# Tying the later modulation's multiplications behind a retention step's own VectorE work

## The chip, the cores and the metric

The kernel runs on one core of one Trainium2 chip. The metric is the device time of one execution in microseconds (us), and lower is better. A core has five engines that run side by side, each through its own queue of instructions in a fixed order: TensorE (PE in the profile, with its weight loads as PEld), VectorE (DVE), ScalarE (ACT), GpSimd (POOL) and SyncE (SP), which here issues most of the DMAs. An engine that waits for a semaphore holds up everything behind the waiting instruction in its own queue.

## The reference, cut to what matters

The reference is one block of a network on 2048 tokens of width 1024. A modulation vector is computed from a conditioning vector `c`, and it is cut into six parts that shift, scale and gate the two halves of the block. The first half mixes tokens with eight heads: four gated linear recurrences (HGRN2) and four retention heads. The second half is a feed-forward part with a short convolution.

```
mod_x = silu(c) @ w_mod + b_mod            # 6 x 1024 values
sh1, sc1, g1, sh2, sc2, g2 = split(mod_x, 6)
hx = rmsnorm(x, norm1_g) * (1 + sc1) + sh1
...                                        # retention, chunk by chunk, per head:
scores = (q_chunk @ k_chunk.T) * intra
o      = scores @ v_chunk + (q_chunk * q_dec) @ r
r      = chunk_dec * r + (k_chunk * k_dec).T @ v_chunk
...
x = x + g1 * (mixed @ w_out)
hx2 = rmsnorm(x, norm2_g) * (1 + sc2) + sh2
x = x + g2 * conv_ffn(hx2)
```

Only `sh1` and `sc1` are needed before the heads. The other four parts, `g1`, `sh2`, `sc2` and `g2`, are needed after them.

## The kernel before, in words

The modulation is computed in twelve stripes of 512 columns. Stripes 0 to 3 (`sh1`, `sc1`) are made at the start. Stripes 4 to 11 are made later, by `mod_later`, while the retention heads run. A stripe is a sum over 1024 rows of `w_mod`, and its rows come in eight tiles of 128 rows. VectorE multiplies each tile by a column of `silu(c)` and adds it to the accumulator `macc` (lines 287 and 289), which is one `tensor_scalar` and seven `scalar_tensor_tensor` for a stripe. Then `mod_rows` sums over the 128 partitions with four small TensorE products (line 232), and line 235 adds the bias. `macc` has one buffer, so a stripe begins when the stripe before it has been summed up. The tiles `wm` have four buffers (tag `q`), so the load of a tile (line 278, on SyncE's queue) waits until the tile four before it has been multiplied.

The heads run one after the other, `h` from 0 to 7, and the last four are retention heads (4 to 7). Each head goes through four steps `i` of 512 tokens. A step (written (h, i) below) weaves three things together: `ret_sweep1` of this head, `ret_sweep2` of the head before it, and the projection `ret_proj` for the next step. In `ret_sweep1`, TensorE makes the scores `rsc` (line 1201), VectorE multiplies them with the decay into `rA` (line 1203), TensorE makes four state increments `rup` (line 1119), and then the running state is carried through four chunks: TensorE multiplies with the state (`rob`, line 1221), and VectorE makes the next state (`Kt`, and `rSb` for the last chunk, line 1223). After this line 1227 scales and adds. In `ret_proj`, TensorE's long products `pa`, `pb`, `pc` are taken from PSUM by lines 578 and 586 (VectorE) and by ScalarE; the query and key are then turned by position: a DMA swaps partitions, GpSimd multiplies by the sine (line 1188), and VectorE does lines 1191 and 1192, without which the next step's `rsc` cannot start.

`tick` is called twice in a step, once after the first three pieces of `ret_sweep1` and once at its end. It runs the compute parts whose loads the tick before has started, and starts the next loads. In heads 4, 5 and 6 a tick takes two weight items (preparation of the next head's weights, line 644 among others) and two items of `mod_later`. An item is two tiles. So half a stripe is written down at each tick: stripe 4 at the second tick of (4, 0) and the first of (4, 1), stripe 5 at the second of (4, 1) and the first of (4, 2), stripe 6 at the second of (4, 2) and in the flush ahead of (4, 3). Head 5 does the same with stripes 7, 8 and 9, and head 6 with stripes 10 and 11, which end at the first tick of (6, 2).

The order in which a tick is written down is not the order on the engine. The framework's scheduler plays the program through a timing model of its own while it builds it, and puts an instruction on its engine's queue when the model says that it can start; of several that can start, the one written down first goes first. An instruction whose inputs are ready early can so be queued ahead of work that was written down before it. `issue_after(ins)` adds an edge to each instruction of its block that runs on the engine of `ins`: it is queued behind `ins`. It adds no wait on the chip, since an engine works in the order of its queue. The kernel has one such edge already, at line 1190: line 1191 is queued behind the last `whole` of the projection.

Of the kernel before, what the change touches and what calls it, by code (L numbers as in the profile page):

```python
# [15 lines left out]
ALU = mybir.AluOpType  # L16
PSUM = bass.MemoryType.PSUM

P = 128
# [27 lines left out]
def view(t, off, dims):  # L47
    return bass.AP(t.tensor, t.offset + off, [t.ap[0]] + dims)


class Kern:
# [215 lines left out]
    def mod_later(self, j4):  # L267

        nc = self.nc
        wsrc = self.I["w_mod"][0].rearrange("(k p) n -> p k n", p=P)  # L270
        st = {}

        def item(k0):
            def load():

                st[k0] = w = [self.slot_tile([P, 512], F32, "q", "wm") for _ in range(2)]
                for kk in range(2):
                    nc.sync.dma_start(w[kk], wsrc[:, k0 + kk, 512 * j4:512 * j4 + 512])

            def comp():  # L280
                if k0 == 0:
                    st["acc"] = self.slot_tile([P, 512], F32, "FG", "macc")
                acc, w = st["acc"], st[k0]
                for kk in range(2):
                    c = self.silc[:, k0 + kk:k0 + kk + 1]
                    if k0 + kk == 0:
                        ins = nc.vector.tensor_scalar(acc, w[kk], c, None, ALU.mult)
                    else:
                        ins = nc.vector.scalar_tensor_tensor(acc, w[kk], c, acc, ALU.mult, ALU.add)

                if k0 + 2 == KT:
                    self.mod_rows(acc, 1, j4)
            return load, comp
        return [item(k0) for k0 in range(0, KT, 2)]
# [900 lines left out]
    def ret_sweep1(self, pool, h, g, slot, pr, st):  # L1195
        nc = self.nc
        qk, V = pr["qk"], pr["V"]
        sc = self.ps("sc", [P, 4, P], "rsc")
        for c in range(4):
            cs = slice(c * P, (c + 1) * P)  # L1200
            nc.tensor.matmul(sc[:, c], qk[:, 1, cs], qk[:, 0, cs], start=True, stop=True, skip_group_check=True)
        A = pool.tile([P, 4, P], F32, tag="A", bufs=2, name="rA")
        nc.vector.tensor_tensor(A, sc, view(self.Dm, h * P, [[0, 4], [1, P]]), ALU.mult)
        yield
        Kt = self.slot_tile([P, 2, 4, P], F32, "KTt", "Kt")
        ups = yield from self.ret_increments(h, qk[:, 1], V, Kt)
        ou, qf = self.slot_tiles(slot)
        nc.scalar.copy(qf, qk[:, 0])
        Uf = ou[:, 1].rearrange("p (c t) -> p c t", t=P)
        for i in range(2):  # L1210
            nc.scalar.copy(Uf[:, 2 * i:2 * i + 2], ups[i][:, :, 0])
        op = self.ps("sc", [P, 4, P], "rop")
        for c in range(4):
            nc.tensor.matmul(op[:, c], A[:, c], V[:, c], start=True, stop=True, skip_group_check=True)
        opart = ou[:, 0].rearrange("p (c t) -> p c t", t=P)
        nc.scalar.copy(opart, op)
        yield
        ob = self.ps("sc", [P, 4, P], "rob")
        Sb = st["Sb"]
        for c in (3, 2, 1, 0):  # L1220
            nc.tensor.matmul(ob[:, c], qk[:, 0, c * P:(c + 1) * P], Sb, start=True, stop=True, skip_group_check=True)
            S2 = Kt[:, 0, c] if c else pool.tile([P, P], F32, tag="S1", bufs=2, name="rSb")
            nc.vector.scalar_tensor_tensor(S2, Sb, self.cd[:, 1, h:h + 1], ups[c // 2][:, c % 2, 1], ALU.mult, ALU.add)
            Sb = S2
            yield
        st["Sb"] = Sb
        nc.vector.scalar_tensor_tensor(opart, ob, self.qd[:, 1, h:h + 1], opart, ALU.mult, ALU.add)
        st["grp"][g] = dict(qf=qf, Uf=Uf, T128=view(self.cd, h, [[NH, 2], [0, 4]]), op=opart)
# [607 lines left out]
```

## Time and profile before

| | us |
|---|---|
| runs of the kernel | 2736.52, 2742.63, 2743.33 (median 2742.63) |
| profiled execution | 2745.74 |
| its span, first to last instruction | 2743.7 |
| PE busy | 2562.4 (93%) |
| DVE busy | 1835.8 (67%) |
| ACT busy | 1343.5 (49%) |
| POOL busy | 773.9 (28%) |

Times in the profile count from the start of the span. A row of the timeline has the start, the duration, the engine, the line, the operation, what is written and read, the shape, and in brackets how long the engine sat idle before it and which instruction or DMA ended that. A row of the table by stretches has the busy time of each engine with the number of instructions, then the clock granted to TensorE as a share of 2.4 GHz (its other level, 1.2 GHz, is 0.50), then the share of time in which the DMA engines were busy, and GB/s.

### The profile page before, as it was taken

How to read it: one execution, taken by the hardware profiler on the slowest of the kernel's cores; microseconds unless marked ns; L12 is line 12 of the kernel's file. 1: busy time of each engine (PE TensorE's matmuls, PEld its weight loads, DVE VectorE, ACT ScalarE, POOL GpSimd, SP SyncE). 2: the span in 40 equal slices, each digit the busy share in tenths (PEclk: the TensorE clock that was granted, in tenths of full speed). 3: DMA queues.
4: the chain of work that ended last, by engine and by line, in shares of the span. 5: the costliest groups of instructions: out<-in, count | busy, mean ns of one | idle time of the engine just before them, and what ended most of it. 6: DMA issues, size and time to landing. Idle time of an engine off the chain costs nothing.

```text
span 2743.7 us, 56410 instructions
## 1 busy us (share of the span) xinstructions
PE 2562.4 (93%) x22829; PEld 1692.0 (62%) x22829; DVE 1835.8 (67%) x3569; ACT 1343.5 (49%) x2902; POOL 773.9 (28%) x905
## 2 busy tenths in 40 slices
PE   5789998999998989898999899999999999999998
PEld 2678887889888888787445344444444444444443
DVE  4998676775856666547464888778877777423553
ACT  5776456564544434336354665555555554411220
POOL 3742111220312132121244344344434433000101
PEclk7899999999999999999999999999999999999999
DMA  8224333343447766666532132333233234734552
GB/s 294 102 86 155 123 103 121 101 129 109 148 159 224 227 212 204 215 181 219 194 110 78 50 123 100 112 115 101 99 115 103 98 110 161 272 144 169 207 192 100
DMA packets 216693, 402.37 MB, mean 147 GB/s; under 512 B 16623, under 2 KB 98771, under 8 KB 211824
## 3 DMA queue, kind: packets, MB, share of 16 engines
q1 hardware_dynamic: 203808, 373.42, 40.1%
q10 hardware_dynamic: 12320, 25.18, 3.1%
q8 instruction: 178, 2.92, 0.4%
q14 instruction: 83, 0.68, 0.1%
q0 software_dynamic: 304, 0.17, 0.0%
HBM read 298.57 MB, written 91.75 MB: 142 GB/s over the span
## 4 chain that ended last, share of the span: by engine, by line
PE 63%; DVE 17%; DMA 7%; issue 6%; ACT 4%; POOL 3%; ACTq 0%; DVEq 0%; SPq 0%; POOLq 0%
PE pa L84 7%; PE pa L85 7%; PE pa L86 7%; PE pd L84 5%; PE pd L86 5%; PE pd L85 5%; PE pc L84 3%; PE pc L85 3%; PE pc L86 3%; PE pb L84 2%; PE pb L86 2%; PE pb L85 2%; PE opp L85 2%; PE opp L84 2%; PE opp L86 2%
## 5 line engine op out<-in xcount | busy, mean ns | idle before, releaser
L84 PE MATMUL pa<-feat,w 128*128 128x512 f16 x704 | 267.7, 380 | 8.6 <-ACT ta L544 8.0
L85 PE MATMUL pa<-feat,w 128*128 128x512 f16 x704 | 267.3, 380 | 1.1 <-DVE feat L1367 1.1
L86 PE MATMUL pa<-feat,w 128*128 128x512 f16 x704 | 263.9, 380 | 0.0
L85 PE MATMUL pd<-wd,actl 128*128 128x512 f16 x616 | 233.3, 379 | 0.0
L86 PE MATMUL pd<-wd,actl 128*128 128x512 f16 x616 | 233.3, 379 | 0.0
L84 PE MATMUL pd<-wd,actl 128*128 128x512 f16 x616 | 232.6, 379 | 0.1
L85 PEld LDWEIGHTS <-w 128*128 128x128 f16 x1232 | 120.8, 98 | 152.7 <-issue 12.9
L86 PEld LDWEIGHTS <-w 128*128 128x128 f16 x1232 | 121.4, 99 | 149.1 <-DVE w L644 2.9
L84 PEld LDWEIGHTS <-w 128*128 128x128 f16 x1232 | 121.7, 99 | 140.8 <-issue 1.6
L85 PEld LDWEIGHTS <-hx 128*128 128x128 f16 x1824 | 184.6, 101 | 11.7 <-issue 9.7
L86 PEld LDWEIGHTS <-hx 128*128 128x128 f16 x1824 | 184.6, 101 | 3.0 <-issue 1.9
L84 PEld LDWEIGHTS <-hx 128*128 128x128 f16 x1824 | 184.6, 101 | 2.4
L1592 DVE SCALAR_TENSOR_TENSOR st<-act,modT,st 128x512 f16<-128x512 f32 x154 | 142.9, 957 | 31.6 <-ACT st L1591 30.7
L84 PE MATMUL pa<-w_vg,hx 128*128 128x128 f16 x800 | 148.2, 224 | 5.5 <-DVE cb L578 4.6
L86 PE MATMUL pa<-w_vg,hx 128*128 128x128 f16 x800 | 148.2, 225 | 0.0
L85 PE MATMUL pa<-w_vg,hx 128*128 128x128 f16 x800 | 148.2, 224 | 0.0
L1591 ACT ACTIVATE st<-act,modT 128x512 f16<-128x512 f32 x154 | 107.5, 718 | 80.9 <-DVE act L1581 29.3
L86 PE MATMUL pc<-feat,w 128*128 128x512 f16 x352 | 134.1, 381 | 2.4 <-DVE w L644 2.4
L84 PE MATMUL pc<-feat,w 128*128 128x512 f16 x352 | 133.9, 380 | 2.3 <-ACT feat L1366 1.3
L85 PE MATMUL pc<-feat,w 128*128 128x512 f16 x352 | 133.9, 380 | 0.0
L84 PE MATMUL pa<-hx,w_z 128*128 128x256 f16 x464 | 128.7, 277 | 4.6 <-DVE K L586 2.1
L85 PEld LDWEIGHTS <-w_z 128*128 128x128 f16 x1072 | 108.7, 101 | 34.9 <-issue 23.0
(550 smaller groups left out, 7576.4 us busy)
## 6 DMA issues: line engine op xcount, KB each, us to landing
hx<-hxd SPq DMA_DIRECT2D x212, 512.0 KB, 5.0
actd<-st SPq DMA_DIRECT2D x154, 256.0 KB, 2.0
actl<-actd SPq DMA_DIRECT2D x28, 1024.0 KB, 5.1
wur<-in_w_up_dram SPq DMA_DIRECT2D x44, 512.0 KB, 4.1
raw<-in_w_in_dram SPq DMA_DIRECT2D x36, 512.0 KB, 4.3
wm<-in_w_mod_dram SPq DMA_DIRECT2D x64, 256.0 KB, 4.7
hxd<-hx SPq DMA_DIRECT2D x28, 512.0 KB, 3.4
wdb<-in_w_down_dram SPq DMA_DIRECT2D x44, 256.0 KB, 4.0
```

Of the source, the lines that this page charges most:

```text
L84: mm(ps, lhs(0), rhs(0), start=start, stop=False, skip_group_check=True)
L85: mm(ps, lhs(0), rhs(1), start=False, stop=False, skip_group_check=True)
L86: mm(ps, lhs(1), rhs(0), start=False, stop=stop, skip_group_check=True)
L1591: nc.scalar.activation(p[:, 0], v, AF.Copy, scale=s)
L1592: nc.vector.scalar_tensor_tensor(p[:, 1], v, s, p[:, 0], ALU.mult, ALU.subtract)
```

## The change

The two multiplications of an item are put in an `issue_after` block. The instruction that they are tied to is kept in `self.mark`. `ret_sweep1` sets it when it writes down line 1203 (`rA`), and again at each of the four state updates of line 1223. At the first tick of a step the mark is therefore this step's `rA`, and at the second tick its last state update `rSb`. In the flush ahead of (h, 3) it is the `rSb` of (h, 2). Line numbers after the first hunk move on by one.

```diff
                 acc, w = st["acc"], st[k0]
-                for kk in range(2):
-                    c = self.silc[:, k0 + kk:k0 + kk + 1]
-                    if k0 + kk == 0:
-                        ins = nc.vector.tensor_scalar(acc, w[kk], c, None, ALU.mult)
-                    else:
-                        ins = nc.vector.scalar_tensor_tensor(acc, w[kk], c, acc, ALU.mult, ALU.add)
-
+
+                with self.tc.issue_after(self.mark.ins):
+                    for kk in range(2):
+                        c = self.silc[:, k0 + kk:k0 + kk + 1]
+                        if k0 + kk == 0:
+                            nc.vector.tensor_scalar(acc, w[kk], c, None, ALU.mult)
+                        else:
+                            nc.vector.scalar_tensor_tensor(acc, w[kk], c, acc, ALU.mult, ALU.add)
                 if k0 + 2 == KT:
                     self.mod_rows(acc, 1, j4)
...
-        nc.vector.tensor_tensor(A, sc, view(self.Dm, h * P, [[0, 4], [1, P]]), ALU.mult)
+        self.mark = nc.vector.tensor_tensor(A, sc, view(self.Dm, h * P, [[0, 4], [1, P]]), ALU.mult)
...
-            nc.vector.scalar_tensor_tensor(S2, Sb, self.cd[:, 1, h:h + 1], ups[c // 2][:, c % 2, 1], ALU.mult, ALU.add)
+            self.mark = nc.vector.scalar_tensor_tensor(S2, Sb, self.cd[:, 1, h:h + 1], ups[c // 2][:, c % 2, 1], ALU.mult, ALU.add)
```

## Rows read from the trace of the kernel before

**Rows 1.** The table by stretches: the stage in which the later modulation is multiplied (from the last step of the HGRN2 heads into the first step of head 7), and the last half of the kernel. Columns: stretch, its length, PE, PEld, DVE, ACT and POOL busy (instructions), granted clock, DMA share, GB/s.

```profile
770.70:1220.00 449.30, 402.92 (x4802) 378.56 (x4800) 267.06 (x516) 182.99 (x463) 96.45 (x112) 0.95 0.66 208
1370.00:2743.70 1373.70, 1349.23 (x6640) 628.23 (x6638) 913.61 (x1512) 631.27 (x1133) 427.49 (x447) 0.99 0.37 128
```

**Rows 2.** The same table by step, from one `rA` to the next: from (4, 1) to (4, 2), with stripe 5 in it, and from (6, 0) to (6, 1), with no stripe in it.

```profile
830.20:864.87 34.67, 29.83 (x337) 28.06 (x336) 21.06 (x38) 14.63 (x34) 10.17 (x11) 0.95 0.69 213
1058.60:1090.39 31.79, 31.79 (x411) 30.76 (x410) 17.12 (x43) 13.80 (x40) 4.36 (x7) 1.00 0.51 159
```

**Rows 3.** The view of the tile `macc`: the multiplications (least, median and longest in ns, first and last start in us), and what VectorE waited for ahead of them (us in all, times).

```profile
L289 DVE SCALAR_TENSOR_TENSOR macc<-wm,silc,macc x56: 733/750/1751, 785.8 to 1115.9; 128x512 f32<-128x512 f32 x56
L287 DVE TENSOR_SCALAR macc<-wm,silc x8: 468/480/2471, 784.6 to 1103.0; 128x512 f32<-128x512 f32 x8
  DMA wm<-in_w_mod_dram: 21.7, 13
```

**Rows 4.** The timeline of VectorE in step (4, 1): a multiplication of stripe 5, and the first and the last state update of the step.

```profile
852.15 0.75 DVE L289 SCALAR_TENSOR_TENSOR macc<-wm,silc,macc 128x512 f32<-128x512 f32 x1 [4.20 <-DMA wm<-in_w_mod_dram]
852.82 0.34 DVE L1223 SCALAR_TENSOR_TENSOR Kt<-rSb,cd,rup 128x128 f32<-128x128 f32 x1
...
853.96 0.35 DVE L1223 SCALAR_TENSOR_TENSOR rSb<-Kt,cd,rup 128x128 f32<-128x128 f32 x1
```

**Rows 5.** The same in step (6, 1), with stripe 11.

```profile
1110.51 0.75 DVE L289 SCALAR_TENSOR_TENSOR macc<-wm,silc,macc 128x512 f32<-128x512 f32 x1 [4.69 <-DMA wm<-in_w_mod_dram]
...
1112.38 0.34 DVE L1223 SCALAR_TENSOR_TENSOR Kt<-rSb,cd,rup 128x128 f32<-128x128 f32 x1
...
1114.29 0.35 DVE L1223 SCALAR_TENSOR_TENSOR rSb<-Kt,cd,rup 128x128 f32<-128x128 f32 x1
```

**Rows 6.** The timeline of TensorE: the instructions of the stage that ended idle time of TensorE and stand near a stripe.

```profile
853.21 0.87 PE L1221 MATMUL rob<-Kt,K 128*128 128x128 f32 x4 [4.45 <-DVE Kt L1223]
...
894.80 1.79 PE L1201 MATMUL rsc<-K 128*128 128x128 f32 x8 [4.32 <-DVE K L1192]
...
978.10 0.49 PE L1221 MATMUL rob<-Kt,K 128*128 128x128 f32 x2 [1.29 <-DVE Kt L1223]
979.50 0.87 PE L1221 MATMUL rob<-Kt,K 128*128 128x128 f32 x4 [0.90 <-DVE Kt L1223]
...
1023.99 1.37 PE L1201 MATMUL rsc<-K 128*128 128x128 f32 x8 [1.25 <-DVE K L1192]
...
1048.35 0.22 PE L84 MATMUL pa<-w_vg,hx 128*128 128x128 f16 x1 [2.06 <-DVE cb L578]
...
1112.78 0.80 PE L1221 MATMUL rob<-Kt,K 128*128 128x128 f32 x2 [5.68 <-DVE Kt L1223]
```

**Rows 7.** The table by stretches around five of those, for the granted clock (the third column from the end).

```profile
853.90:857.50 3.60, 3.60 (x38) 3.59 (x37) 0.80 (x3) 0.44 (x1) 2.35 (x1) 0.53 1.11 369
...
890.00:898.00 8.00, 3.68 (x21) 2.92 (x19) 8.00 (x9) 4.75 (x10) 5.63 (x3) 0.82 0.66 226
978.00:984.00 6.00, 4.99 (x45) 4.71 (x46) 3.38 (x8) 1.11 (x3) 0.00 (x0) 0.72 1.06 337
1023.00:1029.00 6.00, 5.01 (x30) 4.13 (x31) 6.00 (x9) 1.69 (x3) 2.06 (x1) 0.72 0.39 122
...
1112.00:1117.00 5.00, 3.87 (x26) 3.52 (x27) 4.18 (x9) 0.74 (x2) 0.00 (x0) 0.51 1.05 314
```

**Rows 8.** The timeline of VectorE: the last state update of the first step of heads 4, 5 and 6, each with the longest idle time of VectorE in the 15 us behind it.

```profile
826.87 0.34 DVE L1223 SCALAR_TENSOR_TENSOR rSb<-Kt,cd,rup 128x128 f32<-128x128 f32 x1
...
837.93 1.14 DVE L644 SCALAR_TENSOR_TENSOR w_z<-raw,p2s,w_z 128x512 f16<-128x512 f32 x1 [3.26 <-ACT w_z L643]
...
952.95 0.34 DVE L1223 SCALAR_TENSOR_TENSOR rSb<-Kt,cd,rup 128x128 f32<-128x128 f32 x1
...
963.73 1.15 DVE L644 SCALAR_TENSOR_TENSOR w_z<-raw,p2s,w_z 128x512 f16<-128x512 f32 x1 [2.77 <-ACT w_z L643]
...
1085.73 0.34 DVE L1223 SCALAR_TENSOR_TENSOR rSb<-Kt,cd,rup 128x128 f32<-128x128 f32 x1
...
1094.18 5.38 DVE L1242 SCALAR_TENSOR_TENSOR ou<-ou,rs_y,gate 128x128 f32<-128x128 f32 x4 [0.66 <-POOL rs_y L72]
```

**Rows 9.** The same, for the first idle time of more than 1 us behind the last state update of the second step of heads 4, 5 and 6.

```profile
856.60 0.42 DVE L578 TENSOR_TENSOR cb<-pa,cb 128x256 f32<-128x256 f32 x1 [2.29 <-PE pa L86]
...
984.78 0.43 DVE L578 TENSOR_TENSOR ct<-pc,ct 128x256 f32<-128x256 f32 x1 [2.98 <-PE pc L86]
...
1118.85 0.42 DVE L578 TENSOR_TENSOR ct<-pc,ct 128x256 f32<-128x256 f32 x1 [1.79 <-PE pc L86]
```

**Rows 10.** Two multiplications of stripe 6 in the timeline of VectorE, and GpSimd's multiplication by the sine in step (4, 1).

```profile
886.94 0.74 DVE L289 SCALAR_TENSOR_TENSOR macc<-wm,silc,macc 128x512 f32<-128x512 f32 x1
...
890.70 1.75 DVE L289 SCALAR_TENSOR_TENSOR macc<-wm,silc,macc 128x512 f32<-128x512 f32 x1
...
855.02 2.35 POOL L1188 TENSOR_TENSOR Q<-Q,sin 128x1024 f32<-128x1024 f32 x1 [12.50 <-issue]
```

**Rows 11.** What SyncE's queue waited for ahead of the loads of `wm` (us in all, times, longest), and the median time from issue to landing of the loads of `wm` and of the projection's inputs `hx` (the last column).

```profile
SPq L278 <- DVE macc L287: 17.9, 6, 6.1
...
wm<-in_w_mod_dram SPq DMA_DIRECT2D x64, 256.0 KB, 4.7
...
hx<-hxd SPq DMA_DIRECT2D x212, 512.0 KB, 5.0
```

## The prediction

> **What bounds the kernel now.** I read the table by stretches first. TensorE is the bound: in the last half it is busy for 1349.23 of 1373.70 us, and in the stage where the change works for 402.92 of 449.30 us [rows 1]. So 46 us of that stage are idle TensorE time, and the mean clock there is 0.95, which gives back up to another 22 us. What follows the stage is TensorE work without slack, so whatever TensorE saves here should arrive at the end. By step, the one that holds stripe 5 has 29.83 us of TensorE work in 34.67 us at clock 0.95, and the one with no stripe is full, 31.79 of 31.79 us at 1.00 [rows 2].
>
> Second, the tile view: 64 multiplications, 0.75 us each, or 0.48 for the first of a stripe, and ahead of them VectorE stood for 21.7 us in 13 waits for the weights' DMA [rows 3]. Third, VectorE's timeline, to see who stood behind those waits. In (4, 1) VectorE sits 4.20 us for a tile of `wm`, and the state update that the head needs runs directly behind it [rows 4]. In (6, 1) it sits 4.69 us, and again the state update is behind [rows 5]. Last, TensorE's timeline: those two steps are where `rob` waits 4.45 and 5.68 us for that state update [rows 6]. The multiplications are needed only after the heads, yet they stand ahead of a chain that TensorE waits for.
>
> **What the change removes.** No work goes: 64 multiplications stay, and so do their loads. An edge costs nothing by itself on an engine that works in queue order. What changes is the position, and I take the places one by one.
>
> Stripe 5: both halves now come behind the `rSb` at 853.96 or the following `rA`, so the 4.45 us wait of `rob` goes. Behind it the clock stands at 0.53 for 3.60 us; at full clock that work is 3.60 x 0.47 = 1.7 us shorter [rows 7]. Together 6.1.
>
> Stripe 6: its eight multiplications stand around line 1192 and the state updates of (4, 2); they now follow this step's `rSb`. TensorE waits 4.32 us there for line 1192 [rows 6]. Of the VectorE time ahead of line 1192, one multiplication holds 0.66 us of queue, by the 0.74 us row, and one 1.67, by the 1.75 us row [rows 10]. That is 2.3 us. The low clock in this stretch costs 8.00 x 0.18 = 1.4 us [rows 7], and since half the gap stays I count half of it. Together 3.0.
>
> Stripe 8: waits of 1.29 and 0.90 us [rows 6], and 6.00 x 0.28 = 1.7 us of clock [rows 7]. Together 3.9.
>
> Stripe 9: a wait of 1.25 us for line 1192 [rows 6] with a multiplication inside the chain, and 1.7 us of clock [rows 7]. Together 2.9.
>
> Stripe 11: a wait of 5.68 us [rows 6] and 5.00 x 0.49 = 2.45 us of clock [rows 7]. Together 8.1.
>
> Stripes 4, 7 and 10 stand far ahead of their new place and I give no gain for them. The wait of 2.06 us behind stripe 10 [rows 6] stays, because stripe 9, queued behind the `rSb` of (5, 2), comes to lie in that place, with the same four buffers and the same eight loads. In the same way stripe 6 takes the place of stripe 7. The sum of the gains is 6.1 + 3.0 + 3.9 + 2.9 + 8.1 = 24.0 us.
>
> **What the new places cost.** A stripe is 0.48 + 7 x 0.75 = 5.7 us of VectorE [rows 3]; the first half is 2.7, the second 3.0.
>
> Stripes 4, 7 and 10 now fall into the stretch behind the `rSb` of (h, 0), where VectorE also prepares weights. The longest pauses in that stretch are 3.26, 2.77 and 0.66 us [rows 8]. What does not fit is 2.4, 2.9 and 5.0 us, together 10.3. Queued behind it are line 644 and the evacuations of line 586, for which TensorE's product banks wait. With three banks in turn TensorE may not notice at all (0), or it may wait for all of it (10.3). I take half, 5.
>
> Here the two halves are also close together: `rA` of (4, 1) follows `rSb` of (4, 0) by 830.20 - 826.87 = 3.3 us [rows 2, 8], and a load of `wm` lands 4.7 us after its issue [rows 11], which the first half has to release. So a DMA wait between 0 and 4.7 us can come back in each of the three places, 0 to 14.1 us together, now ahead of weight preparation and not of the state chain. The earlier waits were 21.7 / 13 = 1.7 us on average [rows 3], and part of it falls in pauses that exist anyway. I take 1 us each, 3.
>
> Stripes 5, 8 and 11 come in behind the `rSb` of (h, 1), where pauses of 2.29, 2.98 and 1.79 us wait for the first half's 2.7 [rows 9]. What is over is 0.4 + 0 + 0.9 = 1.3 us. The second half follows behind the next `rA`, 864.87 - 853.96 = 10.9 us later [rows 2, 4], with its loads landed, in a stretch where VectorE waits for projections. Beside GpSimd a multiplication took 1.75 in place of 0.75 us [rows 10], and GpSimd's sine product of 2.35 us starts about a microsecond behind the `rSb` of (4, 1) [rows 10]. So the cost lies between 0 and 1.3 + 3 x 1.0 = 4.3, and I take 2.
>
> The Trainium skill bears on that last cost ("SBUF — State Buffer", section "Who interferes with whom"): a VectorE instruction with two SBUF inputs and a GpSimd instruction that reads SBUF exclude each other for the whole instruction, and whichever issues first makes the other wait in full. These multiplications read the tile and the accumulator, both in SBUF, and the 1.75 us row agrees with a wait of that kind. By the rule a multiplication that comes behind the start of the sine product would wait for its whole 2.35 us, in three places 7.1 us, and the sum would be 5 us worse than mine, still a gain.
>
> The costs are 5 + 3 + 2 = 10, and the net gain is 24.0 - 10 = 14 us. Against the profiled execution, 2745.74 (span 2743.7 and 2.0 us around it), that is 2731.7. The median of the runs lies 3.1 us below that execution, so I predict 2728.6 us.
>
> **The rivals.** *The next wait takes over.* The state chain is free, but TensorE then stops at the following evacuation (lines 578 and 586), because the same 5.7 us of a stripe now stand ahead of that one. For it speaks the row at 1048.35, where TensorE waited 2.06 us for line 578 and not for the state [rows 6]. Against it speak the pauses behind the second steps [rows 9]. The costs are then at their upper ends, 10.3 + 4.3 + about 5 of the DMA waits, near 20, and 4 to 5 us are left: about 2738.
>
> *SyncE's queue turns into the bound, and the kernel is slower.* The loads of `wm` stand in one queue with the loads of `hx`. A load whose buffer is released by a multiplication that now sits behind `rSb` holds all `hx` loads behind it. Such holds lasted up to 6.1 us before [rows 11], and `hx` needs 5.0 us to land. The ring has ten tiles and a step takes seven, so three tiles are spare: 3/7 of a step of 31.79 us, 13.6 us, less 5.0 for landing, is about 8.6 us of cover. It decides from a hold of 8.6 us on. If six of the eight stripes hold the queue 5 us beyond that, TensorE loses 30 us and some 1.7 us of clock each time, 40 together; less the gain of 24 that is +16, about 2759 us. Against it: no TensorE wait of the stage ends on an `hx` load now, and the loads are queued late when their multiplication is.
>
> *The edge does not buy what it says.* The scheduler plans everything anew from these positions on, and other VectorE work (line 644, the sums of another head) may be drawn ahead of the state update instead, so the wait stays under another name. Then the time stays within 8 us of the median, 2742.6, on either side.
>
> **How the numbers follow.** I give the forecast 0.55, the taken-over wait 0.20, SyncE's queue 0.15, and the new plan without effect 0.10. A measurement of this kernel can tell about 0.3%, or 8.2 us, from no change: faster ends at 2734.4 and slower begins at 2750.9. The forecast lies in faster except for its worst corner (0.51 of 0.55), and the others add 0.05 and 0.03, so 0.59. Within 0.3% falls 0.04 of the forecast, 0.14 and 0.05 of the two middle cases, 0.23. Slower is the rest, 0.18. The forecast's own range is 2742.6 - 24 - 4 = 2714 to 2740 with all costs at their upper ends. For 8 in 10 it is taken from 2711 to 2750.
>
> **What would show it.** Right: `rob` in (4, 1), (5, 1) and (6, 1) no longer waits over a microsecond for a state update, the clock in those steps is near 1.00, and every multiplication starts behind its `rSb` or `rA`. VectorE's waits for `wm` may stay in number but no state update follows one. The stage from the first `rA` of head 4 to the first of head 7 is some 14 us shorter and the rest of the kernel as long as before. Wrong: TensorE waits of several us for lines 578, 586 or 644 behind a stripe (first rival), TensorE or its weight loads waiting for `hx` (second), or a changed length of the parts ahead of or behind the stage.

## The result and the profile after

The changed kernel takes 2726.78 us, the median of seven runs (2721.92 to 2735.92); the kernel before, run beside it seven times, 2742.63 (2736.52 to 2745.98). The ratio is 0.9943, with a 95% interval of 0.9931 to 0.9956: 0.57% faster, some 16 us. Forecast were 2728.6 us, within 2711 to 2750. All medians below leave out one execution of e11 and one of the kernel before, which took 3728 and 4572 us at a granted clock of 0.65 and 0.58.

The profiled execution took 2735.92, the longest of the seven, so its times understate the gain. A second profile of the same kernel (run e8 below) is of an execution of 2720.64 us, the fastest of its six, and both are read here.

First the table by stretches, with the columns of [rows 1]. The stretch is the stage from the first `rA` of head 4 to the first of head 7. Of the kernel before:

```profile
799.47:1188.88 389.41, 348.67 (x4032) 327.92 (x4031) 234.50 (x453) 161.81 (x413) 89.69 (x110) 0.95 0.66 208
```

The same stage of the changed kernel, then its three steps (h, 1), of which the first and the third answer to the steps of [rows 2, 5]:

```profile
798.38:1176.65 378.27, 342.64 (x4030) 322.10 (x4029) 226.77 (x461) 161.95 (x413) 96.76 (x110) 0.97 0.68 219
830.87:859.33 28.46, 25.89 (x310) 24.03 (x308) 25.57 (x41) 13.40 (x34) 11.59 (x11) 1.00 0.73 239
955.32:985.79 30.47, 27.11 (x320) 25.45 (x319) 23.20 (x44) 13.59 (x31) 11.77 (x11) 0.97 0.77 243
1082.08:1112.92 30.84, 27.34 (x320) 25.55 (x319) 23.45 (x45) 13.69 (x31) 12.00 (x11) 0.96 0.78 233
```

And the stage in the second profile:

```profile
795.08:1164.64 369.56, 337.50 (x4030) 318.87 (x4029) 228.48 (x460) 161.63 (x413) 96.78 (x110) 0.98 0.69 224
```

The stage is 11.1 us shorter in the one trace and 19.9 in the other. What follows it is as long as before: 2743.7 - 1188.88 = 1554.8 us before, 1557.5 and 1554.3 after. Ahead of it the first `rA` of head 4 starts at 799.5 us before, and at 798.4 and 795.1 after. In the stage the columns separate two parts. TensorE's idle time (length less PE busy) fell from 40.7 to 35.6 and 32.1 us. Its busy time for the same matmuls (4030 in these two profiles, 4032 before) fell from 348.67 to 342.64 and 337.50 us, with a granted clock of 0.97 and 0.98 in place of 0.95.

The second part can't be read off one profile each: the two profiles of the changed kernel differ by 5.1 us in it, and e10 below, which gains nothing that can be told, has 342.13 us there. What all executions show is their mean granted clock: 0.9714 on average over the 13 of the change, 0.9689 over 63 of the kernel before, and 0.9691 over the 12 of e10. An estimate from these: 2562.4 us of PE busy x 0.0025 / 0.9714 is 6.6 us, so somewhat under half of the 16 us came back through the clock.

The view of the tile `macc`, which answers to [rows 3]:

```profile
L291 DVE SCALAR_TENSOR_TENSOR macc<-wm,silc,macc x56: 734/747/1751, 827.7 to 1118.4; 128x512 f32<-128x512 f32 x56
L289 DVE TENSOR_SCALAR macc<-wm,silc x8: 478/482/1241, 826.4 to 1099.9; 128x512 f32<-128x512 f32 x8
...
  DMA wm<-in_w_mod_dram: 9.7, 10
```

The multiplications are as many and as long. The first begins 42 us later than before, and VectorE stands idle for their loads for 9.7 us in place of 21.7.

VectorE's timeline in step (6, 1), which answers to [rows 5]:

```profile
1098.50 0.35 DVE L1224 SCALAR_TENSOR_TENSOR Kt<-rSb,cd,rup 128x128 f32<-128x128 f32 x1
...
1099.65 0.35 DVE L1224 SCALAR_TENSOR_TENSOR rSb<-Kt,cd,rup 128x128 f32<-128x128 f32 x1
1099.91 0.48 DVE L289 TENSOR_SCALAR macc<-wm,silc 128x512 f32<-128x512 f32 x1
...
1106.06 1.23 DVE L1192 TENSOR_TENSOR K<-K,cos 128x1024 f32<-128x1024 f32 x1 [1.92 <-DMA Q<-K]
...
1109.52 1.23 DVE L1193 TENSOR_TENSOR K<-K,Q 128x1024 f32<-128x1024 f32 x1 [2.23 <-POOL Q L1189]
...
1115.67 0.75 DVE L291 SCALAR_TENSOR_TENSOR macc<-wm,silc,macc 128x512 f32<-128x512 f32 x1 [0.62 <-DMA wm<-in_w_mod_dram]
```

The state updates come first, and the stripe's first multiplication starts 0.26 us behind the start of the last one, as the edge says. The one wait for `wm` that this stripe has left comes 16 us later, behind the next `rA`, and no state update stands directly behind it.

TensorE's timeline, which answers to [rows 6]:

```profile
847.01 1.25 PE L1222 MATMUL rob<-Kt,K 128*128 128x128 f32 x6 [0.27 <-DVE Kt L1224]
...
973.17 0.83 PE L1222 MATMUL rob<-Kt,K 128*128 128x128 f32 x6
...
983.77 1.98 PE L1202 MATMUL rsc<-K 128*128 128x128 f32 x8 [3.13 <-DVE K L1193]
...
1100.17 0.83 PE L1222 MATMUL rob<-Kt,K 128*128 128x128 f32 x6
...
1110.80 2.08 PE L1202 MATMUL rsc<-K 128*128 128x128 f32 x8 [3.16 <-DVE K L1193]
```

The waits of 4.45, 1.29 and 5.68 us are 0.27, nothing and nothing. The two waits of 3.1 us for line 1193 are new (2.5 and 2.6 us in the second profile): the next thing that TensorE stops at in (5, 1) and (6, 1) is the rotated `K`. By VectorE's rows above, that one is late in (6, 1) for the DMA that makes the rotated copy (1.92) and for GpSimd's product with the sine (2.23), and no multiplication stands in it; (5, 1) has 1.89 and 2.23. The view of the waits from 798 to 1190 us, for TensorE (us in all, times, longest):

```profile
PE rsc L1202 <- DVE K L1193: 7.8, 3, 3.2
PE otp L920 <- DVE ou L935: 7.0, 3, 3.0
PE otp L920 <- DVE ou L1243: 6.3, 3, 3.4
...
PE rob L1222 <- DVE Kt L1224: 1.8, 2, 1.5
```

The same view of the kernel before, from 799 to 1189 us:

```profile
PE rob L1221 <- DVE Kt L1223: 13.5, 7, 5.7
PE rsc L1201 <- DVE K L1192: 6.5, 3, 4.3
PE otp L919 <- DVE ou L1242: 4.0, 3, 2.7
...
PE otp L919 <- DVE ou L934: 3.3, 3, 1.7
```

So the waits for the state update fell by 11.7 us, but idle time by 5.1 alone. Most of the difference is at `otp`, the transposed output of a head: its waits for lines 935 and 1243 rose from 7.3 to 13.3 us (10.8 in the second profile). Ahead of the three longest of these, VectorE itself sat idle for 2.3 to 5.3 us until GpSimd's line 72 was done, and no multiplication stood there. Why they come out longer here was not tested.

### The profile page after: what moved, and what is told of

It is laid out like the page before. It is cut to its first block, busy times and chain, and to the rows that moved or that the text cites. A ratio compares the mean times of both kernels' runs of the same rounds, so it can differ in the third digit from the quotient of the medians.

```text
span 2734.1 us, 56424 instructions
## 1 busy us (share of the span) xinstructions
PE 2557.4 (94%) x22829; PEld 1686.3 (62%) x22829; DVE 1821.8 (67%) x3569; ACT 1343.0 (49%) x2902; POOL 779.3 (29%) x905
## 4 chain that ended last, share of the span: by engine, by line
PE 61%; DVE 15%; DMA 8%; issue 7%; ACT 4%; POOL 4%; ACTq 1%; SPq 0%; POOLq 0%; DVEq 0%
PE pa L84 6%; PE pa L85 6%; PE pa L86 6%; PE pd L86 5%; PE pd L84 5%; PE pd L85 5%; DMA Q<-K 3%; PE pc L84 3%; PE pc L85 3%; PE pc L86 3%; PE pb L84 2%; PE pb L86 2%; PE pb L85 2%; PE opp L84 2%; PE opp L85 2%
## 5 line engine op out<-in xcount | busy, mean ns | idle before, releaser
L85 PEld LDWEIGHTS <-hx 128*128 128x128 f16 x1824 | 182.0, 100 | 9.5 <-issue 7.3
L86 PEld LDWEIGHTS <-hx 128*128 128x128 f16 x1824 | 182.1, 100 | 2.8 <-issue 1.9
L84 PEld LDWEIGHTS <-hx 128*128 128x128 f16 x1824 | 182.4, 100 | 2.3
L1593 DVE SCALAR_TENSOR_TENSOR st<-act,modT,st 128x512 f16<-128x512 f32 x154 | 144.3, 967 | 32.1 <-ACT st L1592 32.1
L84 PE MATMUL pa<-w_vg,hx 128*128 128x128 f16 x800 | 145.2, 222 | 2.9 <-DVE cb L579 2.3
L85 PE MATMUL pa<-w_vg,hx 128*128 128x128 f16 x800 | 144.9, 222 | 0.0
L86 PE MATMUL pa<-w_vg,hx 128*128 128x128 f16 x800 | 144.8, 222 | 0.0
```

The costliest lines, as they stand in the source:

```text
L84: mm(ps, lhs(0), rhs(0), start=start, stop=False, skip_group_check=True)
L85: mm(ps, lhs(0), rhs(1), start=False, stop=False, skip_group_check=True)
L86: mm(ps, lhs(1), rhs(0), start=False, stop=stop, skip_group_check=True)
L1593: nc.vector.scalar_tensor_tensor(p[:, 1], v, s, p[:, 0], ALU.mult, ALU.subtract)
```

## The experiments

Theory at the outset: the gain is the wait of the state update behind a DMA, in the steps (h, 1), for stripes 5, 8 and 11, with a smaller part from 6 and 9; stripes 4, 7 and 10 only cost. Rival A: stripes 4, 7 and 10 carry the gain. Rival B: the edge of any stripe gives a new plan (the order in which the scheduler puts instructions on the queues), and the new plan is what gains. Rival C: it is the VectorE time of the multiplications ahead of the chain, and not the wait.

| run | median, us | ratio to before | stage, us | `rob` waits for `Kt`, us |
|---|---|---|---|---|
| before | 2742.63 | | 389.4 | 13.5 |
| the change | 2726.78 | 0.9943 [0.9931, 0.9956] | 378.3 | 1.8 |
| e8, the change again | 2729.6 | 0.9942 [0.9928, 0.9957] | 369.6 | 1.8 |
| e1, no mark at the state update | 2740.32 | 0.999 [0.998, 1.000] | 385.5 | 3.4 |
| e2, no mark at `rA` | 2729.95 | 0.9948 [0.993, 0.9965] | 374.6 | 0.3 |
| e3, edge for 5, 8, 11 | 2726.98 | 0.994 [0.9927, 0.9954] | 378.2 | 0.8 |
| e4, edge for all but 4, 7, 10 | 2729.67 | 0.995 [0.9934, 0.9965] | 372.4 | none |
| e5, edge for 4, 7, 10 | 2729.24 | 0.9945 [0.9933, 0.9957] | 376.2 | 8.4 |
| e10, edge for 6, 9 | 2739.61 | 0.9991 [0.9978, 1.0005] | 384.0 | 17.0 |
| e11, edge for 5, 11 | 2732.63 | 0.9967 [0.9954, 0.998] | 380.5 | 6.3 |
| e6, before with half the loads | 2723.53 | 0.9927 [0.9914, 0.994] | 371.7 | 3.2 |
| e9, the change with half the loads | 2723.37 | 0.9933 [0.9918, 0.9948] | 369.4 | 2.8 |
| e7, before with few multiplications | 2740.24 | 0.9988 [0.998, 0.9997] | 376.0 | 0.7 |
| e12, the change with few multiplications | 2723.01 | 0.9919 [0.9904, 0.9933] | 374.7 | 4.1 |

The stage (from `rA` of (4, 0) to that of (7, 0)) and the waits are those of the one profiled execution, and two of one kernel differ by 8.7 us in the stage; verdicts rest on the ratios and on single waits. The kernel before, run beside e1 to e12, had medians of 2742.17 to 2744.01.

**Which mark is it (e1, e2).**

```diff
-            self.mark = nc.vector.scalar_tensor_tensor(S2, Sb, ...)
+            nc.vector.scalar_tensor_tensor(S2, Sb, ...)
```

> The change with one part undone: only line 1203 (rA) sets the mark, the state updates do not. My theory (the gain is that no multiplication stands ahead of a state update that TensorE waits for): the multiplications of stripes 5, 8 and 11 are then tied to rA alone and come back ahead of the state updates, so most of the gain is lost, 2736 to 2746 us, ratio to the kernel before 0.998 to 1.001, and TensorE waits several us for a state update again. Rival A (the gain is that stripes 4, 7 and 10 no longer run early, in the head before): they stay behind an rA here, so the gain stays, about 2727 us, 0.994. Rival B (any edge makes the scheduler plan anew, and the gain is the luck of that plan): anywhere within 8 us of the kernel before, with no relation to the waits for the state update.

e2 does the same to the mark at `rA`.

> The change with the other part undone: only the state updates set the mark, so the items of a step's first tick are tied to the rSb of the step before and not to this step's rA. My theory: no multiplication can come ahead of a state update of its step's second tick, so the time is that of the change, 2723 to 2731 us, 0.993 to 0.996. Rival A: the same. Rival B: anywhere within 8 us of the kernel before.

Without the mark at the state update the gain is gone (0.999); with it alone it is whole (0.9948). But e1 lost it by other waits than those of before, and not as its forecast said. Its `rob` waits once for more than a microsecond, 3.4 us in (4, 2). TensorE's timeline of e1:

```profile
975.27 0.27 PE L84 MATMUL pa<-w_vg,hx 128*128 128x128 f16 x1 [4.13 <-ACT ct L547]
```

ScalarE's timeline of e1, which says what held line 547 (a row with ACTq is the issue of a DMA on ScalarE's queue):

```profile
972.57 2.13 ACTq L1169 DMA_DIRECT2D Q<-K  x2
974.74 0.47 ACT L547 ACTIVATE ct<-pa,dq 128x256 f32<-128x256 f32 x1 [5.18 <-DMA Q<-K]
```

ScalarE stood 5.18 us behind its own DMA issue, and the evacuation that frees a bank for TensorE stood behind it; 4.43 us of the same kind follow at 1104.88. So e1's time is no measure of the waits that the change removes. It does say that stripes 4, 7 and 10 coming late isn't enough for a gain, against rival A in its plain form, and that a short wait of `rob` isn't enough either.

**Which stripes (e3, e4, e5, e10, e11).** One line, with the set of stripes:

```diff
-                with self.tc.issue_after(self.mark.ins):
+                with self.tc.issue_after(self.mark.ins) if j4 in (5, 8, 11) else ExitStack():
```

> The edge for stripes 5, 8 and 11 alone; the others stay free. My theory: by the prediction's own sum these three give 6.1 + 3.9 + 8.1 = 18.1 us and cost 2, so about 2727 us, 0.994, with the waits of rob in (4, 1), (5, 1) and (6, 1) gone. Rival A: stripes 4, 7 and 10 stay early, so no gain, 2739 to 2746 us, 0.999 to 1.001. Rival B: anywhere within 8 us of the kernel before.

> The edge for stripes 5, 6, 8, 9 and 11; stripes 4, 7 and 10 stay free. My theory: the gains are 24 us and the costs of stripes 4, 7 and 10 in the stretch of weight preparation (5 + 3 us by the prediction) fall away, so about 22 us faster than the kernel before, 2721 us, 0.992, which beats the change. Rival A: no gain, 2739 to 2746 us. Rival B: anywhere within 8 us of the kernel before.

> The edge for stripes 4, 7 and 10 alone, the complement of the runs before. My theory: these stripes gain nothing by moving and cost up to 8 us in the stretch of weight preparation, and the multiplications of stripes 5, 8 and 11 stay ahead of the state updates: 2740 to 2751 us, 0.999 to 1.003. Rival A (the gain is that these three no longer run early): about 2727 us, 0.994.

> The edge for stripes 6 and 9 alone. Stripes 5 and 11 keep their place ahead of the state updates of (4, 1) and (6, 1), where the DMA waits of 4.20 and 4.69 us were. My theory (what costs is a DMA wait ahead of a state update): at most the 6 us that the prediction gave for stripes 6 and 9, so 2737 to 2744 us, 0.998 to 1.000, with rob waiting 3 us or more for a state update in (4, 1) and (6, 1). Rival B (any edge changes the plan, and nearly any plan is better than that of the kernel before): 2726 to 2732 us, 0.994 to 0.996, as the four other sets of edges had.

> The edge for stripes 5 and 11 alone, the two with the long waits. My theory: the two waits of rob go and the rest stays, by the prediction's sum 6.1 + 8.1 = 14.2 us less 1 to 2 of cost: 2729 to 2734 us, 0.995 to 0.997, with the waits of stripe 8 in (5, 1) as before. If the three parts of the prediction's sum really add, this lies 4 us above the run with stripes 5, 8 and 11. Rival B: anywhere from 2724 to 2744 us.

Stripes 5, 8 and 11 alone give all of it (0.994). Stripes 6 and 9 alone give nothing that can be told (0.9991), though their plan is new too, so rival B falls in the form that any new plan gains. In e10's VectorE and TensorE timelines the old pattern stands, as in [rows 4, 6]. VectorE of e10 in (4, 1):

```profile
849.98 0.75 DVE L291 SCALAR_TENSOR_TENSOR macc<-wm,silc,macc 128x512 f32<-128x512 f32 x1 [4.52 <-DMA wm<-in_w_mod_dram]
850.64 0.34 DVE L1224 SCALAR_TENSOR_TENSOR Kt<-rSb,cd,rup 128x128 f32<-128x128 f32 x1
```

TensorE of e10, in (4, 1), (5, 1) and (6, 1):

```profile
851.04 1.15 PE L1222 MATMUL rob<-Kt,K 128*128 128x128 f32 x4 [4.77 <-DVE Kt L1224]
...
976.17 0.80 PE L1222 MATMUL rob<-Kt,K 128*128 128x128 f32 x2 [5.27 <-DVE Kt L1224]
...
1109.39 2.15 PE L1222 MATMUL rob<-Kt,K 128*128 128x128 f32 x6 [5.95 <-DVE Kt L1224]
```

In (5, 1) the wait is longer than before (1.29 and 0.90 us in [rows 6]).

In e11 stripe 8 has no edge, and the wait stays in its step alone. VectorE of e11:

```profile
974.82 0.75 DVE L291 SCALAR_TENSOR_TENSOR macc<-wm,silc,macc 128x512 f32<-128x512 f32 x1 [3.54 <-DMA wm<-in_w_mod_dram]
...
976.98 0.34 DVE L1224 SCALAR_TENSOR_TENSOR Kt<-rSb,cd,rup 128x128 f32<-128x128 f32 x1
```

TensorE of e11:

```profile
977.37 0.80 PE L1222 MATMUL rob<-Kt,K 128*128 128x128 f32 x2 [4.82 <-DVE Kt L1224]
```

A 3.54 us wait of VectorE became one of 4.82 of TensorE, and e11 is 5.7 us above e3. One such wait, with the clock behind it, is worth about that; by the two intervals the difference is uncertain by 5 us.

Two forecasts failed here. e4 was to beat the change by leaving 4, 7 and 10 where they were; it is level with it. TensorE's waits of e4 in the stage show what it pays:

```profile
PE pa L84 <- DVE cb L579: 9.0, 4, 3.3
```

These waits are 2.6 us before (line 578 there), 5.0 in e3, and there are none in the change.

And e5, which ties only 4, 7 and 10 and was to gain nothing, gains as much as the change. Its VectorE timeline in (6, 1) shows how, beside [rows 5]:

```profile
1092.02 1.42 DVE L289 TENSOR_SCALAR macc<-wm,silc 128x512 f32<-128x512 f32 x1
...
1093.48 0.75 DVE L291 SCALAR_TENSOR_TENSOR macc<-wm,silc,macc 128x512 f32<-128x512 f32 x1
...
1095.20 0.74 DVE L291 SCALAR_TENSOR_TENSOR macc<-wm,silc,macc 128x512 f32<-128x512 f32 x1
...
1096.53 0.75 DVE L291 SCALAR_TENSOR_TENSOR macc<-wm,silc,macc 128x512 f32<-128x512 f32 x1
1097.19 0.34 DVE L1224 SCALAR_TENSOR_TENSOR Kt<-rSb,cd,rup 128x128 f32<-128x128 f32 x1
1097.57 0.73 DVE L1224 SCALAR_TENSOR_TENSOR Kt<-Kt,cd,rup 128x128 f32<-128x128 f32 x2
1100.83 2.67 DVE L291 SCALAR_TENSOR_TENSOR macc<-wm,silc,macc 128x512 f32<-128x512 f32 x1 [2.53 <-DMA wm<-in_w_mod_dram]
1103.42 0.33 DVE L1224 SCALAR_TENSOR_TENSOR rSb<-Kt,cd,rup 128x128 f32<-128x128 f32 x1
```

And TensorE behind it:

```profile
1105.46 0.22 PE L84 MATMUL pa<-w_vg,hx 128*128 128x128 f16 x1 [3.29 <-DVE cb L579]
```

Stripe 11 has no edge here and still begins ahead of the state update. But only four of its multiplications do, as many as there are tiles of `wm`, and all four find their data landed. The fifth, which must wait for a reload, falls behind the first three updates (`Kt`), which are those that this step's `rob` reads, and the wait (2.53 us) with it. The last update, `rSb`, still stands behind that wait, but the next step alone reads it. The kernel before had six ahead. So the edge on a stripe isn't needed to spare `rob` the wait: it is enough that its fifth multiplication comes behind the three updates. The wait isn't free there: line 579 stands behind it, and TensorE waits 3.29 us for that (2.43 in (5, 1)), less than the 5.68 of before. Why the plan moved by that much is argued only: `macc` has one buffer, a stripe begins when the one before it has been read, and that one was late. e5 pays in other places too, above all a wait of 5.20 us of `rob` in (5, 2), where stripe 9's untied multiplications and weight preparation lie in the chain, and is level all the same. The waits of its one profile don't add up to a gain of 15 us: idle time in the stage is 36.8 us against 40.7. Rival A is thus right in that 4, 7 and 10 can carry the gain, but their coming late is not enough by itself (e1).

**The wait or the work (e6, e9, e7, e12).** In e6, on the kernel before, each item loads one tile and multiplies it twice, so that half the loads go and all 64 multiplications stay. e9 is the same edit on the change.

```diff
-                st[k0] = w = [self.slot_tile([P, 512], F32, "q", "wm") for _ in range(2)]
-                for kk in range(2):
+                st[k0] = w = [self.slot_tile([P, 512], F32, "q", "wm")] * 2
+                for kk in range(1):
                     nc.sync.dma_start(w[kk], wsrc[:, k0 + kk, 512 * j4:512 * j4 + 512])
```

> The kernel before, with no edge, but each item loads one tile of the later modulation and multiplies it twice (every second tile of w_mod is left out of stripes 4 to 11). The multiplications keep their number and, nearly, their places, but four buffers now hold four items, so a multiplication hardly waits for its DMA. If the cost was the DMA wait ahead of the state update (my theory's larger part: gaps of 4.45 and 5.68 us follow waits of 4.20 and 4.69 us): 8 to 14 us faster than the kernel before, 2729 to 2735 us, 0.995 to 0.997. If the place alone is what costs, whatever the wait: 2739 to 2746 us, 0.999 to 1.001. It also has half the load traffic of these stripes, which may add a little.

> The change, and besides each item loads one tile and multiplies it twice (every second tile of w_mod is left out of stripes 4 to 11). It is the control for the run with half the loads and no edge, which had both no DMA wait ahead of a state update and less load traffic. If that run gained by the waits alone, there is nothing left to gain here, since the change has put the waits behind the state update: within 6 us of the change, 2721 to 2733 us, 0.992 to 0.996. If it gained by the traffic, the change gains as much again: 2708 to 2718 us, 0.986 to 0.990.

VectorE of e6 in (6, 1):

```profile
1091.08 0.47 DVE L287 TENSOR_SCALAR macc<-wm,silc 128x512 f32<-128x512 f32 x1
...
1091.59 3.90 DVE L289 SCALAR_TENSOR_TENSOR macc<-wm,silc,macc 128x512 f32<-128x512 f32 x5
1095.41 0.34 DVE L1223 SCALAR_TENSOR_TENSOR Kt<-rSb,cd,rup 128x128 f32<-128x128 f32 x1
```

TensorE's waits of e6 in the stage:

```profile
PE rob L1221 <- DVE Kt L1223: 3.2, 7, 0.6
```

At the state updates this decides against rival C. Six multiplications still stand ahead of the update, with no edge anywhere, and they cost TensorE at most 0.6 us at a time. What went is the wait for their data, and the time is 0.9927 of before. That is more than was forecast for e6 (2729 to 2735 us; it takes 2723.53), and more than the waits of `rob` account for, which are 10.3 us shorter.

In (4, 2) it is otherwise. VectorE and TensorE of e6 there:

```profile
883.67 1.75 DVE L289 SCALAR_TENSOR_TENSOR macc<-wm,silc,macc 128x512 f32<-128x512 f32 x1
...
887.77 2.05 PE L1201 MATMUL rsc<-K 128*128 128x128 f32 x8 [4.31 <-DVE K L1192]
```

Stripe 6 still has this multiplication between lines 1191 and 1192. It waits for no load, and yet `rsc` waits 4.31 us for line 1192, as before (4.32 in [rows 6]). In the change this wait is gone. So here it is not a DMA wait of a multiplication that costs, and rival C is not refuted; how much of the wait the multiplication makes up was not tested.

On the change the same edit as in e6 (e9) brings the time to 0.9933, not below e6, and beyond the change by no more than the intervals allow (0.9943, [0.9931, 0.9956]). So e6 gained by the waits; less traffic can't be told to have added anything.

In e7, on the kernel before, and e12, on the change, 48 of the 64 multiplications are left out and the loads stay:

```diff
-                for kk in range(2):
+                for kk in range(2 if k0 == 0 else 0):
                     c = self.silc[:, k0 + kk:k0 + kk + 1]
```

> The kernel before with six of the eight multiplications of each later stripe left out (48 of 64; the loads stay). It is the ceiling of what can be had by placing them: my theory has gains of 24 us plus the 2.06 us wait behind stripe 10 and its clock, so 24 to 30 us faster than the kernel before, 2713 to 2719 us, 0.989 to 0.991. If the change already has all of it, 2727 us.

> The change with six of the eight multiplications of each later stripe left out (48 of 64; the loads stay). The same was left out of the kernel before in an earlier run, but there the instruction order of the feed-forward part came out differently and cost 10 us; here that order is the one of the kernel before. If what costs is the DMA wait ahead of the state update, the change is already at its ceiling and nothing more comes from taking VectorE's 36 us of multiplications away: 2720 to 2731 us, ratio to the kernel before 0.992 to 0.996. If their own time and place still cost what the prediction put down (10 us), 2710 to 2719 us, 0.988 to 0.991.

e7 is no ceiling. Its stage is 13.4 us shorter and yet its time only 0.9988 of before, because the up half of the feed-forward part, far behind, grew from 840.8 to 850.4 us. That is against both of its forecasts. The order there differs: of ScalarE's 853 operations in that part, 166 are others than before at the same place. The changed kernel has 44 such places and e12 none, and both have that part about as long as before (841.1 and 838.4 us). That the order is the cause is not shown. The 0.9919 of e12 says about what is to be had from these multiplications: 22 us of the kernel before (18 to 26 by the interval), of which the change takes 16. It is no strict bound, since e12 has a plan of its own, with waits of 2.54 us for a state update and 2.17 us for a load of `hx`.

**The change again (e8).**

> The change itself, once more, on the chip of these runs, for the comparison and for a second trace: 2722 to 2731 us, 0.993 to 0.996. In the first trace the profiled execution was the longest of seven (2735.92 against a median of 2726.78); a trace near the median should show the same waits and the difference elsewhere.

The time is the same in another set of runs (0.9942), and its trace is the second one read above.

## Why the prediction was right, point by point

*What bounds the kernel, and the wait that goes.* Right. `rob` no longer waits over a microsecond for a state update in (4, 1), (5, 1) and (6, 1), e10 and e11 put these waits back with their stripes, and e6 shows that it is the DMA ahead and not the place of the multiplications. The clock in these steps is 1.00, 0.97 and 0.96.

*Stripes 5, 8 and 11, 6.1 + 3.9 + 8.1 = 18.1 us.* About right: e3 alone measures 16.5 (2743.49 - 2726.98), costs included. The clock was held to give back 1.7 to 2.5 us behind each wait. These terms multiply the whole length of a stretch in [rows 7], where only TensorE's busy time runs slower: with 4.99, 5.01 and 3.87 us busy they are 1.4, 1.4 and 1.9 us in place of 1.7, 1.7 and 2.45, and stripe 6's half of 1.4 is half of 0.7. That takes 1.5 us off the sum of 24. With stripe 5's 1.7 the five clock terms are then 6.7 us, and the estimate from all executions above is 6.6.

*Stripes 6 and 9, 3.0 + 2.9 us.* Not shown to add anything. e10 has 2.5 us by the ratio, with an interval that reaches past nothing, and e4 with them is not faster than e3 without. The terms were added as if each wait were independent of the others. They are not. In e10 the waits of `rsc` for line 1193 fall to 2.3 us from 6.5 (with 2.0 more for a ScalarE operation), but `rob` waits 17.0 us in place of 13.5, most of the rise in (5, 1). In the change, `rsc` no longer waits in (4, 2) and (5, 2), where these terms were, but it does in (5, 1) and (6, 1), and the sum is 7.8 us.

*Stripes 4, 7 and 10: no gain, and 5 + 3 us of costs.* This is the step that failed. e5 gives them a gain of 15 us (2744.01 - 2729.24); there the fifth multiplication of the next stripe falls behind the three updates. And e4, without them, is no faster than the change, so no net cost of theirs can be seen. What they give where the others are tied shows at line 579: the 2.06 us wait behind stripe 10, which was to stay, is gone in the change, while e4, where stripe 10 still runs early, has 3.26 us in that place, behind a DMA wait of 4.21 us of VectorE for that stripe, and 9.0 in all.

*The third cost, 2 us, for stripes 5, 8 and 11 beside GpSimd.* Not measured by itself. All the costs of the multiplications' time together are, as near as a run shows them, the distance to e12: 0.9943 - 0.9919 = 0.0024, 6.6 us, with an uncertainty nearly as large, where the prediction had 10. In (4, 1) no multiplication met the sine product: three of the first half ran before it and the fourth after it. The operation that met it is line 1192. VectorE's timeline of the change:

```profile
849.47 1.53 DVE L291 SCALAR_TENSOR_TENSOR macc<-wm,silc,macc 128x512 f32<-128x512 f32 x2
...
851.39 3.21 DVE L1192 TENSOR_TENSOR K<-K,cos 128x1024 f32<-128x1024 f32 x1
```

GpSimd's timeline beside it:

```profile
851.16 2.35 POOL L1189 TENSOR_TENSOR Q<-Q,sin 128x1024 f32<-128x1024 f32 x1 [7.10 <-DMA Q<-K]
```

Line 1192 takes 3.21 us in place of the 1.23 of step (6, 1). The sine product ends at 853.51, 2.12 us behind the start of line 1192, and 2.12 + 1.23 is 3.35: a wait for nearly the whole of the rest. The rule of the Trainium skill that the prediction cites ("SBUF — State Buffer", "Who interferes with whom") agrees. It fell on another instruction than the prediction priced.

In (6, 1) the order is the other way round. Line 1192 starts at 1106.06 and takes its 1.23 us, and the sine product, 0.04 us behind it, is the longer one:

```profile
1106.10 3.38 POOL L1189 TENSOR_TENSOR Q<-Q,sin 128x1024 f32<-128x1024 f32 x1 [9.41 <-DMA Q<-K]
```

That is 1.03 us more than the 2.35 of (4, 1), and (5, 1) has 3.39. Line 1193 waits for this product, so by this estimate a microsecond of each of the new 3.1 us waits of `rsc` comes from the meeting of these two, which no term of the prediction had.

*The net.* 24 less 10 gave 14; measured were 16. By e12, gains and costs were rather 22 and 6: both sums a few us too large, within what these intervals can tell, with errors that cancel. The total was right, its division among the stripes was not, so that its closeness (14 against 16) is in part luck.

*The rivals.* The next wait does take over, in part: 3.13 and 3.16 us at `rsc` and 6.0 us more at `otp`, where lines 578 and 586 had been named. Line 578 (579 after) does take over in e3, e4 and e5, with 5.0, 9.0 and 6.3 us. SyncE's queue did not become a bound: ahead of the loads of `wm` it waits 37.7 us for multiplications in the stage against 42.6 (the view of SyncE's waits, lines 289 and 291 against 287 and 289), the longest 4.8 against the 6.1 of [rows 11], and no wait of TensorE there ends on an `hx` load. That the edge doesn't buy what it says is refuted by the rows of `rob`.

## What to carry to other kernels

On an engine that works in queue order, look for an operation with time to spare that waits for a DMA directly ahead of one that the bounding engine waits for. The price at the state updates was the wait and not the operation's busy time (e6), and the gain was had by an order that lets the urgent one go first (e3), or by data that has landed (e6; here four tiles for eight multiplications were the limit). Gains of single stripes don't add up: three of the eight carried all of it, and another three could carry it too, so price such a change by the waits that end and by what waits next, not stripe by stripe. And an order is planned as a whole: e1 lost the gain to a wait on another engine.

## What the runs showed of the hardware that was not expected

A DMA issue can hold the compute of the engine that issues it: in e1 ScalarE stood 5.18 us with two issues of line 1169 ahead of its evacuation, 2.13 us of them in the issues themselves; what the issues waited for in the rest is not shown. Where VectorE's line 1192 and GpSimd's sine product meet, the one that starts second is the longer: 3.21 in place of 1.23 us for line 1192 in (4, 1), 3.38 in place of 2.35 for the product in (6, 1). And two executions of one kernel differed by 15.2 us of span (2734.1 and 2718.9), of which 8.7 lie in a stage of 370 us, so that a single profile tells which waits there are better than what they are worth.

A larger number of tiles for `wm` was not tried.
